# RMSNorm on one core: the second tile loaded in halves, the third stored whole, seven rows a group on GpSimd, one ScalarE table

## The chip, the cores and the metric

One Trainium2 chip, one of its cores. The metric is device time in microseconds (us).

## The reference

```python
batch, seq, dim = 16, 1024, 512
x = randn(batch, seq, dim) float32;  gamma = ones(dim) float32
rms = sqrt(mean(x ** 2, axis=-1, keepdims=True) + 1e-5)
out = x / rms * gamma
```

The input is 33.55 MB and so is the output: 67.1 MB in all, with very little arithmetic per byte.

## The kernel before

The 16384 rows are four tiles of 128 partitions x 32 rows x 512 elements (8.4 MB each) in three slots on the chip; tile 3 goes into the slot of tile 0. Work is cut into groups of up to 16 rows. ScalarE squares a piece of a group, VectorE sums it, ScalarE takes the square root, VectorE the reciprocal. Then the rows are shared: GpSimd multiplies the last `share` rows by their factors and by gamma; ScalarE scales the others and VectorE multiplies these by gamma. SyncE issues all transfers, in program order, on one queue.

```python
    load(0, 0, 0, 8)
    # (gamma in five small pieces)
    load(0, 0, 8, 16)
    load(0, 0, 16, 32)
    load(1, 1, 0, 32)
    # ...
    groups = [                         # tile, first row, rows, pieces, share of GpSimd
        (0, 0, 7, (7,), 2),
        (0, 7, 9, (4, 5), 4),
        (0, 16, 16, (7, 5, 4), 7),
        (1, 0, 16, (7, 5, 4), 8),
        (1, 16, 16, (7, 5, 4), 8),
        (2, 0, 16, (7, 5, 4), 8),
        (2, 16, 16, (7, 5, 4), 7),
        (3, 0, 16, (7, 5, 4), 7),
        (3, 16, 16, (7, 5, 4), 3),
    ]
    # ...
    def transfers(t, g):               # issued when a group's code is through
        if (t, g) == (0, 0):
            store(0, 0, 0, 1)
            load(2, 2, 0, 16)
            store(0, 0, 1, 2)
            load(2, 2, 16, 24)
            store(0, 0, 2, 3)
            load(2, 2, 24, 32)
        elif (t, g) == (0, 16):
            store(0, 0, 3, 16)
            store(0, 0, 16, 32)
            load(3, 0, 0, 16)
            load(3, 0, 16, 32)
        elif (t, g) == (1, 16):
            store(1, 1, 0, 32)
        elif (t, g) == (2, 0):
            store(2, 2, 0, 16)
        elif (t, g) == (2, 16):
            store(2, 2, 16, 32)
        elif (t, g) == (3, 0):
            store(3, 0, 0, 16)
        elif (t, g) == (3, 16):
            store(3, 0, 16, 32)
    # ...
    for k, group in enumerate(groups):
        # ... (mine = rows not given to GpSimd, half = half of them, ahead = the next group)
        scale_by_pool(rstd, t, g, n, share)
        for piece in todo[:2]:         # squares and sums of the next group
            square_sums(*piece)
        scale(rstd, t, g, 0, half)
        if not ahead:
            times_gamma(t, g, 0, half)
        for piece in todo[2:]:
            square_sums(*piece)
        scale(rstd, t, g, half, mine)
        times_gamma(t, g, 0 if ahead else half, mine)
        transfers(t, g)
        for nxt in ahead:
            rstd = inverse_rms(ss, nxt[2])
```

## Time and profile before

| | before |
|---|---|
| time, median of the first 3 runs | 161.52 us |
| span of the profiled run | 159.6 us |
| traffic | 67.1 MB, 421 GB/s over the span |
| busiest compute engine | VectorE, 70% |
| transfer engines | 98.2% |

The prediction below shows the busy shares, the stretches, the issues and the chain of waits. Three further readings: The first is SyncE's own waits before it issues (who waited for whom: us in total, times, longest):

```profile
SPq L49 <- DVE slot L115: 52.2, 7, 20.5
SPq L49 <- POOL slot L103: 36.0, 5, 9.2
SPq L45 <- DMA out_dram<-slot: 20.8, 2, 11.1
```

SyncE waits most of the time, for VectorE and GpSimd before stores and for landed stores before loads.

The second is the timeline of SyncE, the stores that matter (start us, duration, line and operation): the first small store, tile 1's, both halves of tile 2's, both of tile 3's.

```profile
27.13 0.35 SPq L49 DMA_DIRECT2D out_dram<-slot  x1
...
92.12 0.34 SPq L49 DMA_DIRECT2D out_dram<-slot  x1
...
108.02 0.34 SPq L49 DMA_DIRECT2D out_dram<-slot  x1
...
121.99 0.33 SPq L49 DMA_DIRECT2D out_dram<-slot  x1
...
135.98 0.33 SPq L49 DMA_DIRECT2D out_dram<-slot  x1
...
142.18 0.33 SPq L49 DMA_DIRECT2D out_dram<-slot  x1
```

The third is the longest wait of a compute engine:

```profile
POOL slot L102 <- DVE ss L96: 32.7, 4, 16.0
```

GpSimd stands 32.7 us, four times, until VectorE has its factors: 16.0 us at the start, and 6.9 us before tile 1, because ScalarE cannot square tile 1 until all 8.4 MB of it have landed.

### The profile page before, as it was taken

To read this page: it belongs to the slowest core of one execution; us is meant where nothing else is said; L and a number is where in the kernel's file an instruction comes from. 1 tells how busy PE (TensorE), PEld (TensorE's weight loads), DVE (VectorE), ACT (ScalarE), POOL (GpSimd) and SP (SyncE) were. 2 spreads that over 40 slices of the span, in tenths; PEclk is the share of its full clock that TensorE was granted. 3 is DMA by queue.
4 is the path that set the end of the run, shared out by engine and by line. 5 is a ranking of instruction groups with operands and counts; after the bars stand their busy time and mean duration, and the time that the engine had idled before them with its cause. 6 is when DMAs were issued, how large, how long until landed. Compare 5 with 4: busy or idle time off the path is not lost.

```text
span 159.6 us, 280 instructions
## 1 busy us (share of the span) xinstructions
PE 2.0 (1%) x2; PEld 0.5 (0%) x2; DVE 111.8 (70%) x43; ACT 108.5 (68%) x110; POOL 108.2 (68%) x24
## 2 busy tenths in 40 slices
PE   0050000000000000000000000000000000000000
PEld 0010000000000000000000000000000000000000
DVE  0027298998069899999999999999999809700000
ACT  3072999960499997989989989999995198000000
POOL 1000731981999309999999999999999999960000
DMA  5999999969799999999999999996999999999995
GB/s 199 419 435 485 435 394 526 526 263 526 329 394 396 454 415 419 427 452 444 476 394 402 509 402 394 526 526 263 526 394 394 394 501 419 394 452 468 394 419 238
DMA packets 2747, 67.12 MB, mean 421 GB/s; under 512 B 313, under 2 KB 314, under 8 KB 698
## 3 DMA queue, kind: packets, MB, share of 16 engines
q1 hardware_dynamic: 2746, 67.11, 98.2%
q14 instruction: 1, 0.01, 0.0%
HBM read 33.56 MB, written 33.55 MB: 421 GB/s over the span
## 4 chain that ended last, share of the span: by engine, by line
POOL 49%; DMA 26%; ACT 8%; DVE 3%; POOLq 2%; issue 0%
POOL slot L103 26%; DMA slot<-in_x_dram 26%; POOL slot L102 23%; ACT slot L111 3%; DVE slot L115 3%; ACT sq_psum L89 3%; POOLq L205 2%; ACT sq_sbuf L89 1%; DVE ss L96 0%; POOLq L102 0%
## 5 line engine op out<-in xcount | busy, mean ns | idle before, releaser
L102 POOL TENSOR_TENSOR slot<-slot,ss 128x3584 f32<-128x3584 f32 (+4 forms) x9 | 47.8, 5310 | 32.7 <-DVE ss L96 32.7
L90 DVE TENSOR_REDUCE ss<-sq_psum 128x7 f32<-128x3584 f32 (+1 forms) x16 | 49.1, 3066 | 20.1 <-ACT sq_psum L89 20.1
L103 POOL TENSOR_TENSOR slot<-slot,gamma_b 128x3584 f32<-128x3584 f32 (+4 forms) x9 | 60.2, 6692 | 0.7
L111 ACT ACTIVATE slot<-slot,ss 128x512 f32<-128x512 f32 x74 | 46.8, 707 | 4.7 <-DVE ss L96 4.7
L89 ACT ACTIVATE sq_psum<-slot 128x3584 f32<-128x3584 f32 (+1 forms) x16 | 40.2, 2510 | 12.4 <-DMA slot<-in_x_dram 11.0
L115 DVE TENSOR_TENSOR slot<-slot,gamma_psum 128x4608 f32<-128x4608 f32 (+4 forms) x10 | 40.8, 4093 | 4.9 <-ACT slot L111 4.9
L90 DVE TENSOR_REDUCE ss<-sq_sbuf 128x5 f32<-128x2560 f32 x8 | 22.4, 2805 | 0.0
L89 ACT ACTIVATE sq_sbuf<-slot 128x2560 f32<-128x2560 f32 x8 | 18.6, 2323 | 0.0
L95 ACT ACTIVATE ss<-ss,eps_t 128x16 f32<-128x16 f32 (+2 forms) x9 | 2.7, 303 | 4.2 <-DVE ss L90 4.2
L95 ACT ACT_TABLE_LOAD x1 | 1.3, 1283 | 4.0 <-DVE ss L90 4.0
L96 DVE RECIPROCAL ss<-ss 128x16 f32<-128x16 f32 (+2 forms) x9 | 2.1, 235 | 1.7 <-ACT ss L95 1.7
L65 PE MATMUL gamma_psum<-gamma_row,ones_col 1*128 1x512 f32 x2 | 2.0, 1118 | 8.7 <-DMA gamma_row<-in_gamma_dram 8.7
L89 ACT ACT_TABLE_LOAD x1 | 1.3, 1283 | 1.1 <-PEq L194 1.1
L160 ACT COPY gamma_b<-gamma_psum 128x512 f32<-128x512 f32 x1 | 0.6, 566 | 0.0
L65 PEld LDWEIGHTS gamma_psum<-gamma_row,ones_col 1*128 1x128 f32 x2 | 0.5, 308 | 8.7 <-issue 8.7
L63 POOL MEMSET ones_col<- 1x128 f32 x1 | 0.2, 194 | 0.3 <-POOLq L194 0.3
L194 POOL MEMSET const-float32-0.0<- 128x1 f32 x1 | 0.1, 98 | 0.2 <-issue 0.2
L194 POOL MEMSET const-bfloat16-1.0<- 128x1 bf16 x1 | 0.1, 101 | 0.0
L194 POOL MEMSET const-uint8-127<- 128x1 uint8 x1 | 0.1, 101 | 0.0
L194 POOL MEMSET const-float32-1.0<- 128x1 f32 x1 | 0.1, 98 | 0.0
L69 POOL MEMSET eps_t<- 128x1 f32 x1 | 0.1, 88 | 0.0
## 6 DMA issues: line engine op xcount, KB each, us to landing
out_dram<-slot SPq DMA_DIRECT2D x5, 4096.0 KB, 16.6
slot<-in_x_dram SPq DMA_DIRECT2D x4, 4096.0 KB, 19.3
slot<-in_x_dram SPq DMA_DIRECT2D x4, 2048.0 KB, 9.9
out_dram<-slot SPq DMA_DIRECT2D x1, 3328.0 KB, 32.4
out_dram<-slot SPq DMA_DIRECT2D x3, 256.0 KB
gamma_row<-in_gamma_dram SPq DMA_DIRECT2D x4, 0.4 KB
gamma_row<-in_gamma_dram SPq DMA_DIRECT2D x1, 0.5 KB
slot<-in_x_dram SPq DMA_DIRECT2D x1, 34.3
```

The source lines that it names most:

```text
L65: nc.tensor.matmul(gamma_psum[:, 0], ones_col, gamma_row, start=True, stop=True)
L89: nc.scalar.activation(out=sq[:, :m], in_=rows, func=AF.Square)
L90: nc.vector.tensor_reduce(out=ss[:, r : r + m, 0], in_=sq[:, :m], axis=mybir.AxisListType.X, op=OP.add)
L95: nc.scalar.activation(out=ss[:, :n, 0], in_=ss[:, :n, 0], func=AF.Sqrt, bias=eps_t, scale=1.0 / D)
L96: nc.vector.reciprocal(out=ss[:, :n, 0], in_=ss[:, :n, 0])
L102: nc.gpsimd.tensor_tensor(out=part, in0=part, in1=by_row, op=OP.mult)
L103: last = nc.gpsimd.tensor_tensor(out=part, in0=part, in1=gamma_b.to_broadcast([P, share, D]), op=OP.mult)
L111: nc.scalar.activation(out=x[:, g + r, :], in_=x[:, g + r, :], func=AF.Copy, scale=rstd[:, r])
L115: scaled = nc.vector.tensor_tensor(out=part, in0=part, in1=gamma_psum.to_broadcast([P, r1 - r0, D]), op=OP.mult)
L160: nc.scalar.copy(out=gamma_b[:, 0], in_=gamma_psum[:, 0])
L194: nc = _bacc.Bacc("TRN2", target_bir_lowering=False, num_devices=1)
L205: with _tile.TileContext(nc) as tc:
```

## The change

The intent, read from the diff: let compute start on tile 1 when half of it is there; balance GpSimd (15.9 us for a group with eight rows) with VectorE; load ScalarE's table once, in idle time; and with that room spend fewer, larger transfers and instructions (tile 2 stored whole, the last group's multiply in one piece).

```diff
--- before.py
+++ after.py
@@ -57,7 +57,8 @@
         nc.sync.dma_start(out=gamma_row[:, c0:c1], in_=gamma.unsqueeze(0)[:, c0:c1])
     load(0, 0, 8, 16)
     load(0, 0, 16, 32)
-    load(1, 1, 0, 32)
+    load(1, 1, 0, 16)
+    load(1, 1, 16, 32)
 
     ones_col = const.tile([1, P], fp32)
     nc.gpsimd.memset(ones_col, 1.0)
@@ -67,15 +68,17 @@
 
     eps_t = const.tile([P, 1], fp32)
     nc.gpsimd.memset(eps_t, eps)
+    table = const.tile([P, 1], fp32)
+    nc.scalar.activation(out=table, in_=eps_t, func=AF.Sqrt)
 
 
     groups = [
-        (0, 0, 7, (7,), 2),
-        (0, 7, 9, (4, 5), 4),
+        (0, 0, 7, (7,), 3),
+        (0, 7, 9, (4, 5), 5),
         (0, 16, 16, (7, 5, 4), 7),
-        (1, 0, 16, (7, 5, 4), 8),
-        (1, 16, 16, (7, 5, 4), 8),
-        (2, 0, 16, (7, 5, 4), 8),
+        (1, 0, 16, (7, 5, 4), 7),
+        (1, 16, 16, (7, 5, 4), 7),
+        (2, 0, 16, (7, 5, 4), 7),
         (2, 16, 16, (7, 5, 4), 7),
         (3, 0, 16, (7, 5, 4), 7),
         (3, 16, 16, (7, 5, 4), 3),
@@ -134,10 +137,8 @@
             load(3, 0, 16, 32)
         elif (t, g) == (1, 16):
             store(1, 1, 0, 32)
-        elif (t, g) == (2, 0):
-            store(2, 2, 0, 16)
         elif (t, g) == (2, 16):
-            store(2, 2, 16, 32)
+            store(2, 2, 0, 32)
         elif (t, g) == (3, 0):
             store(3, 0, 0, 16)
         elif (t, g) == (3, 16):
@@ -168,12 +169,10 @@
         for piece in todo[:2]:
             square_sums(*piece)
         scale(rstd, t, g, 0, half)
-        if not ahead:
-            times_gamma(t, g, 0, half)
         for piece in todo[2:]:
             square_sums(*piece)
         scale(rstd, t, g, half, mine)
-        times_gamma(t, g, 0 if ahead else half, mine)
+        times_gamma(t, g, 0, mine)
         transfers(t, g)
         for nxt in ahead:
             rstd = inverse_rms(ss, nxt[2])
```

## The prediction

> **What bounds the kernel now.** I read the page's head first, then the stretches, then the DMA queue's own issues and waits, and only last the chain of waits, which here points at the wrong thing.
>
> The page's busy shares, its slices and the DMA totals:
>
> ```profile
> PE 2.0 (1%) x2; PEld 0.5 (0%) x2; DVE 111.8 (70%) x43; ACT 108.5 (68%) x110; POOL 108.2 (68%) x24
> DMA  5999999969799999999999999996999999999995
> q1 hardware_dynamic: 2746, 67.11, 98.2%
> HBM read 33.56 MB, written 33.55 MB: 421 GB/s over the span
> ```
>
> No compute engine passes 70%; the transfer engines are at 98.2%. The two 5s are the first and last slice. The 6s and 7s need a second look, because this row books a packet in the slice where it starts, and a 64 KB packet takes 2.4 us of a 4 us slice. So I asked for busy time by stretch (columns: stretch in us and its length, then each engine's busy time, the clock, the DMA share, GB/s):
>
> ```profile
> 0.00:1.70 1.70, 0.00 (x0) 0.00 (x0) 0.00 (x0) 0.55 (x1) 0.43 (x6) 1.00 0.00 0
> 1.70:158.40 156.70, 2.04 (x2) 0.50 (x2) 111.83 (x43) 107.94 (x110) 107.79 (x18) 1.00 1.00 428
> 158.40:159.60 1.20, 0.00 (x0) 0.00 (x0) 0.00 (x0) 0.00 (x0) 0.00 (x0) 1.00 0.00 0
> ```
>
> From 1.7 us to 158.4 us the share is 1.00: the queue is never dry. The span is 1.7 us until the first packet, 156.7 us of moving 67.11 MB at 428 GB/s, and 1.2 us until the last landing is seen. The profiled run took 161.61 us, 2.0 us more than its 159.6 us span. That is the whole time; no engine is in it.
>
> How far ahead is the queue filled? The issues, with the median time from issue to landing at the right:
>
> ```profile
> out_dram<-slot SPq DMA_DIRECT2D x5, 4096.0 KB, 16.6
> slot<-in_x_dram SPq DMA_DIRECT2D x4, 4096.0 KB, 19.3
> out_dram<-slot SPq DMA_DIRECT2D x1, 3328.0 KB, 32.4
> ```
>
> 4 MiB (4.19 MB) at 428 GB/s is 9.8 us. A store that lands 16.6 us after its issue has stood some 7 us behind others, so issuing it some us later costs nothing.
>
> The chain of waits says something else:
>
> ```profile
> by line: POOL slot L103 26.4%; DMA slot<-in_x_dram 26.0%; POOL slot L102 22.5%; ACT slot L111 3.5%; DVE slot L115 3.1%; ACT sq_psum L89 3.1%; POOLq L205 2.2%; ACT sq_sbuf L89 1.4%; issue 0.3%; DVE ss L96 0.1%; POOLq L102 0.1%
> ```
>
> It follows the last *engine* instruction, a GpSimd multiply that ends at 142.2 us, while the program ends at 159.6 us. Its 49% of GpSimd describes a chain whose output then waits in the queue.
>
> **What the Trainium skill says.** "DMA: Bandwidth & Descriptors", Specifications, gives a fabric ceiling of 435 GB/s for a core's 16 engines. The trace agrees: 428 GB/s over 156.7 us. The same page, Queues, rings and completion order, says that each engine consumes descriptors in ring order; I use this as first-in first-out. "ScalarE: Activation LUTs", What ACT_TABLE_LOAD costs, gives about 1283 ns a load plus a drain; the trace shows two loads of exactly 1283 ns. "GPSIMD Engine Reference", section 3.1, gives 4497 ns for a two-input [...]operation of 2048 fp32 a partition against 2293 ns on VectorE; here the multiply by gamma of that size takes 4513 ns, but the one with the row factor broadcast only 3601 ns, so I use the trace's rows.
>
> **The change part by part.** The rows used (engine operation, form, count, busy, mean ns):
>
> ```profile
> L103 POOL TENSOR_TENSOR slot<-slot,gamma_b 128x4096 f32<-128x4096 f32 x3 | 26.6, 8870 | 0.2
> L103 POOL TENSOR_TENSOR slot<-slot,gamma_b 128x3584 f32<-128x3584 f32 x3 | 23.3, 7776 | 0.2
> L102 POOL TENSOR_TENSOR slot<-slot,ss 128x4096 f32<-128x4096 f32 x3 | 21.0, 7015 | 6.9 <-DVE ss L96 6.9
> L102 POOL TENSOR_TENSOR slot<-slot,ss 128x3584 f32<-128x3584 f32 x3 | 18.5, 6166 | 3.8 <-DVE ss L96 3.8
> L95 ACT ACT_TABLE_LOAD x1 | 1.3, 1283 | 4.0 <-DVE ss L90 4.0
> ```
>
> To see what is on the path I need deadlines: when the queue reaches each transfer. With all bytes ahead of it at 2.335 us per MB (156.7/67.11) from 1.7 us on: the first small store at 41 us (16.8 MB of loads ahead); tile 1's store at 99.6 (41.9 MB); tile 2's at 119.2 (50.3 MB); its second half at 129.0; tile 3's two stores at 138.8 and 148.6. Before, their issues stand in the SyncE timeline at 27.1, 92.1, 108.0, 122.0, 136.0 and 142.2 us: margins of 14, 7.5, 11, 7, 2.8 and 6.4 us, all positive, which is why nothing is dry.
>
> 1. Table. One of two loads goes from the path of the first group (1.28 us) to the idle time before the first data (7.9 us). With three instead of two rows given to GpSimd the first VectorE multiply has four rows instead of five (0.54 us a row). First store issued at about 25 instead of 27.1; deadline 41. Worth 0.
> 2. Tile 1 in halves. ScalarE's square of tile 1 waited until the whole 8 MB landed at 42.2 us. The first half, 12.6 MB in, lands at about 32. ScalarE finishes the preceding work at 36.7, so it saves 5.5 us there, and the reciprocal for tile 1 comes at about 54 instead of 59.9. In bytes nothing changes. The trace's packet records give 2418 ns for 64 KB and 1213 ns for 32 KB: a transfer engine needs 16 x 1213 instead of 8 x 2418 ns, +0.06 us. All transfers are numbered one higher; SyncE issued the ninth only when the first had landed (at 7.9 us), so I read eight semaphores used in turn. The transfers now sharing one lie eight apart and have landed long before. Worth +0.06.
> 3. Seven rows on GpSimd. A group of eight costs 7.02 + 8.87 = 15.9 us, of seven 6.17 + 7.78 = 13.9 us, 2.0 less in each of three groups. VectorE's multiply gains a row, 4.95 instead of 4.41 us; its start-to-start period goes from 13.15 to 13.69 us (the seven-row stretch 99.5 to 113.2 shows it), still below GpSimd. So with tile 1's first reciprocal at 54, GpSimd ends groups at about 68, 82, 96, 110 and 124 us. Tile 1's store is issued at 82 instead of 92.1: it only stands longer. Worth 0.
> 4. Tile 2 stored whole. It must wait for the second half: issued at about 110, against 108.0 for the first half before. Deadline 119.2, margin 9. Packets of 64 KB instead of 32: -0.06 us.
> 5. The last group unsplit. ScalarE's 13 rows take 8.07 us, then VectorE's multiply 7.1 in one, no longer overlapped: issue at about 139 if the group starts at 124; deadline 148.6. Worth 0.
>
> Sum on the path: +0.06 - 0.06 = 0.00. One small chance remains: the last 64 KB packets of tile 1's load took 2785 instead of 2418 ns in the packet records (at 38.7 to 41.6 us, 0.37 us lost on every engine). I don't know the cause; with 32 KB packets it may halve. I allow -0.1: 161.5 - 0.1 = 161.4 us.
>
> **The rivals.** *Compute sets the end.* The chain's reading would give 5.9 (first half) + 3 x 2.0 (seven rows) + about 1.3 (table) = 13 us saved, 148 us. Against it: 67.11 MB at even the page's 435.2 GB/s is 154.2 us, and with the 1.7, 1.2 and 2.0 us outside 159.1 us (an estimate from that page and the trace). No schedule of this traffic is over 1.5% faster.
>
> *The whole store starves the queue.* Had compute kept its pace, the store of tile 2 would be issued at 122.0, 2.8 us after its deadline, plus some 1 us until the first packet (0.74 to 1.75 us at the start): 165.3 us, 2.4% slower. The parts 2 and 3 are there to prevent it. Even if the early half brought nothing, 60.2 + 4 x 14.0 = 116 us still meets 119.2. So both would have to fail.
>
> *The last group becomes the bound.* If it started as before (reciprocal at 126.9), the unsplit end comes at 126.9 + 8.1 + 7.2 = 142.2 us, as before. It would have to slip by 6.4 us to cost anything.
>
> **Range and chances.** Three runs before lie within 0.13 us. The transfers' slow packets and another chip may move it some tenths. 161.4 us, eight times in ten 160.9 to 161.9. Over 2% faster needs 158.3 us or less, below the 159.1 us floor: 0.01. Over 2% slower needs 164.8, about 3.3 us of dry queue, which only the second rival makes, with 9 us of margin against it: 0.01. Within 2%: 0.98.
>
> **What would show it.** Right: the DMA share is again 1.00 from about 1.7 us to the last packet at about 158.3; the gap of 6.9 us before GpSimd's multiply in tile 1 shrinks or goes; one table load, early; tile 1's store issued near 82, landing some 38 us later; tile 2's near 110, landing near 139; the last near 139. Wrong: a stretch of low DMA share near 119 us with SyncE waiting for GpSimd or VectorE there, a second table load between first squares and square root that reaches the first store, or a DMA rate other than 428 GB/s. A time under 159 us would mean that the traffic has another ceiling than I read.

## The result, and the profile after

| | before | after |
|---|---|---|
| time, median of 4 runs each | 161.54 us (161.43 to 161.66) | 161.56 us (161.45 to 161.56) |
| span of the profiled run | 159.6 us | 159.5 us |

The ratio is 0.9999, 95% interval 0.9982 to 1.0017. A ratio is the mean time of one kernel's runs over that of the other's of the same rounds, so not quite the ratio of the medians quoted. The time is the same.

The stretches of the changed kernel, same columns as in the prediction:

```profile
0.00:1.70 1.70, 0.00 (x0) 0.00 (x0) 0.00 (x0) 0.55 (x1) 0.44 (x6) 1.00 0.00 0
1.70:158.40 156.70, 2.04 (x2) 0.49 (x2) 112.55 (x42) 107.60 (x111) 105.96 (x18) 1.00 1.00 428
158.40:159.60 1.20, 0.00 (x0) 0.00 (x0) 0.00 (x0) 0.00 (x0) 0.00 (x0) 1.00 0.00 0
```

The middle stretch is the same 156.7 us at share 1.00 and 428 GB/s. What did change is all in front of the queue. SyncE's timeline, the same stores (tile 2's is one now):

```profile
24.91 0.35 SPq L49 DMA_DIRECT2D out_dram<-slot  x1
...
82.15 0.39 SPq L49 DMA_DIRECT2D out_dram<-slot  x1
...
109.18 0.34 SPq L49 DMA_DIRECT2D out_dram<-slot  x1
...
123.16 0.33 SPq L49 DMA_DIRECT2D out_dram<-slot  x1
...
138.00 0.33 SPq L49 DMA_DIRECT2D out_dram<-slot  x1
```

Tile 1's store is issued 10.0 us sooner, tile 3's first 12.8 us, the last 4.2 us. None of it reaches the end. The last store shows where it goes, issue to landing in us at the right, after:

```profile
out_dram<-slot SPq DMA_DIRECT2D x1, 4096.0 KB, 20.7
```

Before, the last store was issued at 142.18 us and took 16.6 us; 142.18 + 16.6 = 158.8. Now 138.00 + 20.7 = 158.7. The 4.2 us won are spent standing in the queue. The waits of the engines, after:

```profile
POOL slot L105 <- DVE ss L99: 21.7, 4, 14.7
...
ACT sq_psum L92 <- DMA slot<-in_x_dram: 7.0, 2, 5.3
```

GpSimd's wait fell by 11.0 us. ScalarE's table load, two before, is one, in idle time (from the costliest groups):

```profile
L72 ACT ACT_TABLE_LOAD x1 | 1.3, 1283 | 1.1 <-PEq L193 1.1
```

ScalarE waits for data 7.0 us instead of 11.0, and one of its two waits is new: 1.73 us at 91.1 us, for the load of tile 3. Compute has run so far ahead that it now catches up with the loads. The chain of waits has changed entirely: it gave GpSimd 49% before, and none of its 44 pieces is GpSimd's now, while the time is the same.

### The profile page after: what moved, and what is told of

The parts are those of the page before. It is cut to its first block, busy times and chain, and to the rows that moved or that the text cites. A ratio compares the mean times of both kernels' runs of the same rounds, so it can differ in the third digit from the quotient of the medians.

```text
span 159.5 us, 280 instructions
## 1 busy us (share of the span) xinstructions
PE 2.0 (1%) x2; PEld 0.5 (0%) x2; DVE 112.5 (71%) x42; ACT 108.2 (68%) x111; POOL 106.4 (67%) x24
## 4 chain that ended last, share of the span: by engine, by line
DMA 38%; DVE 29%; ACT 16%; issue 2%; ACTq 0%; SPq 0%
DMA out_dram<-slot 22%; DMA slot<-in_x_dram 17%; DVE ss L93 17%; DVE slot L118 12%; ACT slot L114 8%; ACT sq_psum L92 6%; ACT sq_sbuf L92 1%; ACTq L204 0%; ACT ss L98 0%; ACT gamma_b L161 0%; DVE ss L99 0%; SPq L49 0%; ACTq L92 0%
## 5 line engine op out<-in xcount | busy, mean ns | idle before, releaser
L105 POOL TENSOR_TENSOR slot<-slot,ss 128x3584 f32<-128x3584 f32 (+2 forms) x9 | 46.9, 5216 | 21.7 <-DVE ss L99 21.7
L106 POOL TENSOR_TENSOR slot<-slot,gamma_b 128x3584 f32<-128x3584 f32 (+2 forms) x9 | 59.2, 6582 | 0.7
L114 ACT ACTIVATE slot<-slot,ss 128x512 f32<-128x512 f32 x75 | 47.5, 709 | 4.7 <-DVE ss L99 4.7
L118 DVE TENSOR_TENSOR slot<-slot,gamma_psum 128x4608 f32<-128x4608 f32 (+2 forms) x9 | 41.3, 4592 | 8.5 <-ACT slot L114 8.5
```

What stands on the lines that cost most here:

```text
L105: nc.gpsimd.tensor_tensor(out=part, in0=part, in1=by_row, op=OP.mult)
L106: last = nc.gpsimd.tensor_tensor(out=part, in0=part, in1=gamma_b.to_broadcast([P, share, D]), op=OP.mult)
L114: nc.scalar.activation(out=x[:, g + r, :], in_=x[:, g + r, :], func=AF.Copy, scale=rstd[:, r])
L118: scaled = nc.vector.tensor_tensor(out=part, in0=part, in1=gamma_psum.to_broadcast([P, r1 - r0, D]), op=OP.mult)
```

## The experiments

The theory: the transfer queue sets the end. Each transfer has a deadline, the moment at which the queue has finished all before it; an issue well before its deadline costs nothing, one after it costs the lateness plus the time from issue to first packet. Rival 1: the chain of engine work (mostly GpSimd) sets the end. Rival 2: the whole store is harmless in any case, and the other parts have no purpose. Twelve kernels were run: four that do parts of the change alone (a1, a2, a3, d1), three that change GpSimd's work (a4, b4, b3), four with less traffic (b1, b2, c1, c2), and one that changes the order of transfers (c3). The ratio given is to the kernel before in the same rounds.

### a1: tile 2 stored whole, alone

```diff
 # the kernel before
-        elif (t, g) == (2, 0):
-            store(2, 2, 0, 16)
         elif (t, g) == (2, 16):
-            store(2, 2, 16, 32)
+            store(2, 2, 0, 32)
```

> The kernel before with one part of the change alone: tile 2 stored whole after its second half. Theory (the transfer queue sets the end, every transfer has a deadline): compute is as slow as before, so the store is issued at about 122.0 us, while the queue finishes tile 1's store at about 119.4 us; with some 1 us from issue to first packet the queue is dry for about 3.6 us and the time is about 165.1 us (2.2% slower), with a dip in the DMA row near 119 us. Rival 1 (the chain of GpSimd work sets the end): GpSimd does what it did, so 161.5 us. Rival 2 (a whole store is hidden anyway): 161.5 us.

Measured: 165.27 us, ratio 1.0221 (1.0205 to 1.0236), slower. The stretches, and the issue of tile 2's store in SyncE's timeline:

```profile
1.70:119.20 117.50, 2.04 (x2) 0.49 (x2) 96.65 (x38) 97.10 (x93) 84.72 (x14) 1.00 1.00 428
119.40:122.50 3.10, 0.00 (x0) 0.00 (x0) 3.10 (x3) 2.54 (x5) 3.10 (x2) 1.00 0.00 0
122.60:162.20 39.60, 0.00 (x0) 0.00 (x0) 11.78 (x4) 8.07 (x13) 19.68 (x4) 1.00 0.98 424
```

```profile
122.28 0.34 SPq L49 DMA_DIRECT2D out_dram<-slot  x1
```

The packet records (start and length of every packet in the trace) show no transfer from 119.97 to 123.13 us: 0.84 us pass from the issue to the first packet. A dry stretch of 3.2 us in the queue goes with a time 3.6 us longer (165.27 - 161.69). Most of the last 0.4 us is in the packet records too: after the dry stretch the remaining 16.8 MB took 39.0 us, here and in a4 below, and 38.7 us in the kernel before, where the queue did not have to start again. Both rivals said 161.5 us and fall. GpSimd did what it did before, and the kernel is slower.

### a2: whole store and seven rows

```diff
 # a1, and
-        (1, 0, 16, (7, 5, 4), 8),
-        (1, 16, 16, (7, 5, 4), 8),
-        (2, 0, 16, (7, 5, 4), 8),
+        (1, 0, 16, (7, 5, 4), 7),
+        (1, 16, 16, (7, 5, 4), 7),
+        (2, 0, 16, (7, 5, 4), 7),
```

> The kernel before with tile 2 stored whole and seven instead of eight rows on GpSimd in the three groups that had eight; no early half of tile 1, no table part. Theory (queue and deadlines): GpSimd starts tile 1 at about 60.2 us and takes 14.0 us a group, so the store is issued at about 116.2 us, 3 us before the queue is through with tile 1's store: 161.5 us. Rival 1 (GpSimd chain sets the end): about 155.5 us, 2 us less for each of three groups.

Measured: 161.60 us, ratio 1.0014 (0.9972 to 1.0056), the same (one of its four runs took 162.99 us). The store of tile 2 was issued at 116.72 us, 5.6 us sooner than in a1.

### a3: whole store and tile 1 in halves

```diff
 # a1, and
-    load(1, 1, 0, 32)
+    load(1, 1, 0, 16)
+    load(1, 1, 16, 32)
```

> The kernel before with tile 2 stored whole and tile 1 loaded in two halves; GpSimd keeps eight rows. Theory (queue and deadlines): GpSimd starts tile 1 at about 54.5 us and takes three groups of 15.9 us and one of 14.0 us, so the store is issued at about 116.3 us, 3 us before it is needed: 161.5 us. Rival 1 (GpSimd chain sets the end): about 156 us, as the chain starts 5.9 us sooner.

Measured: 161.63 us, ratio 0.9994 (0.9977 to 1.0011), the same. Issue at 116.67 us, again 5.6 us sooner than a1. Either of the two parts is enough to pay for the whole store; together they leave room. (Neither part was run without the whole store; that it is then worth nothing follows from the theory and was not measured.)

### d1: the remaining parts alone

```diff
 # the kernel before
+    table = const.tile([P, 1], fp32)
+    nc.scalar.activation(out=table, in_=eps_t, func=AF.Sqrt)
-        (0, 0, 7, (7,), 2),
-        (0, 7, 9, (4, 5), 4),
+        (0, 0, 7, (7,), 3),
+        (0, 7, 9, (4, 5), 5),
-        if not ahead:
-            times_gamma(t, g, 0, half)
-        times_gamma(t, g, 0 if ahead else half, mine)
+        times_gamma(t, g, 0, mine)
```

> The kernel before with the remaining parts of the change alone: the early table load, three and five rows on GpSimd in the first two groups, and the last group's multiply in one piece; tile 1 is loaded whole, tile 2 stored in two halves, eight rows stay on GpSimd elsewhere. Theory (queue and deadlines): one table load instead of two, the first small store issued at about 24.9 instead of 27.1 us, where it isn't needed until 41 us; the last store is issued at about 142.2 us, as before, 6 us before it is needed: 161.5 us. Rival 1 (the chain of engine work sets the end): the 2 us gained at the start come out, 159.5 us, or the unsplit multiply costs its 3 us, 164.5 us.

Measured: 161.55 us, ratio 0.9999 (0.9982 to 1.0015), the same. The first small store is issued at 25.13 us, 2.0 us sooner than before; the last store at 142.14 us, as before.

### a4 and b4: spending the margin on purpose

```diff
 # the changed kernel; groups (1, 0), (1, 16), (2, 0), (2, 16)
-        (1, 0, 16, (7, 5, 4), 7),
+        (1, 0, 16, (7, 5, 4), 9),    # a4; 8 in b4; likewise in the other three
```

> The changed kernel with nine instead of seven rows on GpSimd in tile 1's and tile 2's groups: the margin of tile 2's store is used up on purpose. Theory (queue and deadlines): a group costs GpSimd about 17.9 us, from 53.1 us on four of them end at about 124.7 us, 5.3 us after the queue is through with tile 1's store; with 1 us to the first packet the time is about 167.8 us (3.9% slower), not the 15.6 us that the four groups become longer. Rival 1 (GpSimd chain sets the end): about 177 us.

> The changed kernel with eight instead of seven rows on GpSimd in tile 1's and tile 2's groups. Theory (queue and deadlines): four groups of 15.9 us from 53.1 us end at about 116.8 us, 2.6 us before the queue needs the store: 161.5 us, although GpSimd's groups are 7.8 us longer in sum. Rival 1 (GpSimd chain sets the end): about 169 us.

Measured: nine rows 167.59 us, ratio 1.0368 (1.0352 to 1.0383), slower; eight rows 161.43 us, ratio 0.9974 (0.9946 to 1.0002), the same. SyncE's issue of tile 2's store, in the timeline of b4 and then of a4, and the dry stretch of a4:

```profile
116.97 0.34 SPq L49 DMA_DIRECT2D out_dram<-slot  x1
```

```profile
124.60 0.34 SPq L49 DMA_DIRECT2D out_dram<-slot  x1
```

```profile
119.40:124.90 5.50, 0.00 (x0) 0.00 (x0) 1.83 (x2) 3.63 (x6) 5.50 (x2) 1.00 0.00 0
```

Against the changed kernel's 109.18 us, eight rows cost 7.8 us of GpSimd time and nothing of the end; nine rows cost 15.4 us and 5.9 us of the end (167.59 - 161.69, the kernel before in the same rounds). The packet records of a4 show the queue empty from 119.78 to 125.44 us, 5.7 us. So the curve is flat up to an issue at 116.97 us. Between a1 and a4, run in the same rounds, the issue comes 2.32 us later and the time is 2.32 us longer: slope one. No run has an issue between 117.0 and 122.3 us, so the corner itself was not measured; as 0.84 us pass before the first packet, it must lie that much before the deadline, at about 119 us (an estimate). The deadline itself, 119.8 to 120.0 us, is nearly the same in a1 and a4; the prediction had worked out 119.2.

### b3: GpSimd's multiply by gamma left out

```diff
 # the changed kernel (gamma is one here, so the output stays right; not a valid kernel)
-        nc.gpsimd.tensor_tensor(out=part, in0=part, in1=by_row, op=OP.mult)
-        last = nc.gpsimd.tensor_tensor(
-            out=part, in0=part, in1=gamma_b.to_broadcast([P, share, D]), op=OP.mult
-        )
+        last = nc.gpsimd.tensor_tensor(out=part, in0=part, in1=by_row, op=OP.mult)
```

> The changed kernel without GpSimd's multiply by gamma (59 us of GpSimd work less; gamma is one in these inputs, so that the output stays right here, but it is no valid kernel). Theory (queue sets the end): 161.5 us, the DMA share stays 1.00 from 1.7 to 158.4 us. Rival 1 (the chain of engine work sets the end): over 5 us less.

Measured: 161.62 us, ratio 0.9986 (0.9958 to 1.0014), the same. Its middle stretch (GpSimd's busy time, 46.92 us, stands just before the clock), and GpSimd's longest wait:

```profile
1.70:158.40 156.70, 2.04 (x2) 0.49 (x2) 112.53 (x42) 107.54 (x111) 46.92 (x9) 1.00 1.00 428
```

```profile
POOL slot L105 <- DVE ss L99: 70.1, 8, 14.9
```

59 us of GpSimd work are gone, and the queue's share and rate are the same (1.00 and 428 GB/s): here GpSimd's work did not slow the transfers. But b3 is a weak test of rival 1. GpSimd now waits 70.1 us for VectorE's factors (21.7 in the changed kernel), and tile 2's store is issued at 108.84 us, only 0.3 us sooner, the last one at 137.90, 0.1 us sooner: VectorE, with 13.7 us a group against GpSimd's 14.0, held the pace, so compute hardly ended sooner. What rules out a chain of compute as the end is the changed kernel itself (last store 4.2 us sooner, nothing gained), a2 and a3 (5.6 us sooner than in a1, and only a1's 3.6 us came back) and b4 (7.8 us later, nothing lost).

### b1 and b2: less traffic

If the queue hides the gain, a lighter queue must show it. Both kernels without one store:

```diff
         elif (t, g) == (0, 16):
             store(0, 0, 3, 16)
-            store(0, 0, 16, 32)      # wrong output on purpose: these rows are never written
             load(3, 0, 0, 16)
```

> The kernel before without the store of tile 0's second half (4.19 MB less traffic; part of the output is wrong on purpose). Theory (queue and deadlines): every later transfer could move up by 9.8 us, but the issues for tile 1, the halves of tile 2 and tile 3 come at 92.1, 108.0, 122.0, 136.0 and 142.2 us; the store of tile 3's first half at 136.0 us finds the queue dry, so the end is 136.0 + 1.0 + 2 x 9.8 + 1.2 = 157.8 us of span and about 159.8 us of time: only 1.8 of the 9.8 us come out. A kernel bound by its queue alone would take 151.7 us; a kernel bound by compute alone 161.5 us.

> The changed kernel with the same cut (tile 0's second half is not stored, wrong on purpose). Theory (queue and deadlines): its issues at 82.2, 109.2, 122.5 and 138.0 us all meet the earlier deadlines but for a dry stretch of some 1.6 us before tile 3's load, so the time is about 154.3 us, 3.5% below the kernel before with the same cut: the gain in compute that the full traffic hides. Rival (the change gains nothing in compute worth having): as the kernel before with the cut, about 159.8 us.

Measured: the kernel before with the cut 159.73 us, the changed one with the cut 155.66 us. Their outputs are wrong, as meant. The change is now worth 4.1 us (155.75/159.73 by the means: 2.5%). Stretches of the kernel before with the cut:

```profile
71.30:72.50 1.20, 0.00 (x0) 0.00 (x0) 1.20 (x1) 1.20 (x2) 1.20 (x1) 1.00 0.00 0
122.40:122.90 0.50, 0.00 (x0) 0.00 (x0) 0.50 (x1) 0.00 (x0) 0.50 (x1) 1.00 0.00 0
132.90:136.90 4.00, 0.00 (x0) 0.00 (x0) 4.00 (x2) 2.28 (x4) 4.00 (x2) 1.00 0.00 0
```

Three dry stretches, the longest right before tile 3's first store, issued at 136.13 us. With the change only the first is left (tile 3's load must wait until tile 0's rows have landed outside); behind it the queue of b2 runs to its end:

```profile
72.70:152.30 79.60, 0.00 (x0) 0.00 (x0) 55.91 (x20) 49.69 (x57) 56.31 (x10) 1.00 0.99 419
```

b2's rival (no gain in compute worth having) falls. But I had expected 154.3 us for b2, 1.4 us less. In its packet records the last packets of tile 3's load, at 90 to 92.4 us, took longer, 1.27 us on the mean transfer engine; this accounts for the size of the miss, and its cause is open. With full traffic the same place loses 0.2 us or less.

### c1 and c2: what two parts are worth where compute matters

```diff
 # b2 (the changed kernel, lighter traffic), and
 # c1:
-    load(1, 1, 0, 16)
-    load(1, 1, 16, 32)
+    load(1, 1, 0, 32)
 # c2, in groups (1, 0), (1, 16), (2, 0):
-        (1, 0, 16, (7, 5, 4), 7),
+        (1, 0, 16, (7, 5, 4), 8),
```

> The changed kernel with the lighter traffic (tile 0's second half not stored, wrong on purpose), and tile 1 loaded whole again: what the early half is worth where compute matters. With the lighter traffic the changed kernel took 155.7 us, and its queue was through with tile 1's store at about 112.5 to 113.5 us. Theory (queue and deadlines): without the early half tile 2's store is issued 5.9 us later, at about 115.1 us instead of 109.2, so the queue is dry until about 116.0 us and the time is 116.0 + 38.9 (16.8 MB) + 1.2 + 2.0 = about 158.1 us. Rival (the early half never matters): 155.7 us.

> The changed kernel with the lighter traffic (wrong on purpose), and eight instead of seven rows on GpSimd in the three groups that had eight before. Theory (queue and deadlines): the groups end at 53.1 + 3 x 15.9 + 14.0 = 114.9 us, so tile 2's store is 5.7 us later and the time about 157.9 us, where with the full traffic eight rows cost nothing. Rival (seven rows never matter): 155.7 us.

Measured: c1 159.41 us, c2 157.93 us, against 155.66 us for b2 (another chip; the kernel before took 161.60 and 161.65 us beside them). Tile 2's store was issued at 116.21 us in c1 and 115.10 us in c2, against 109.24 us in b2. Both parts matter where the traffic is lighter. c2 is as expected. c1 is 1.3 us over, and 1.1 of it is the early half: it moves tile 2's store by 7.0 us, not 5.9. The traces show why. With the table load gone and more rows on GpSimd in the first groups, ScalarE was ready for tile 1 at 35.2 us in the changed kernel, not at 36.7 us as before, so a whole load holds it longer: in c1 it stood 6.65 us (until 42.16), where it had stood 5.56 us in the kernel before.

### c3: all loads first

The changed kernel's queue still loses some tenths at about 38 us, when tile 1's load ends and the first small store begins. I tried to take that switch away:

```diff
 # the changed kernel
     load(1, 1, 16, 32)
+    load(2, 2, 0, 32)
 # (the three small stores and tile 2's three loads at (0, 0) are gone)
-            store(0, 0, 3, 16)
+            store(0, 0, 0, 16)
```

> The changed kernel with full traffic, tile 2's load as one transfer right behind tile 1's, and the first sixteen rows of tile 0 stored as one transfer after it (three small stores of 256 KB gone, so one switch of the queue from loads to stores less). Theory (the queue sets the end, and its only losses are packets that take longer at such switches, 0.3 us near 38 us, and the short packets of the small stores, some 0.15 us): about 161.1 us, 0.3% less, not over 0.6%. Rival (those losses do not come from the switch or are taken again elsewhere): 161.5 us.

Measured: 162.56 us, ratio 1.0066 (1.0050 to 1.0083): 0.7% slower where I had expected 0.3% less, clear of noise. Stretches:

```profile
1.70:58.00 56.30, 2.04 (x2) 0.49 (x2) 41.17 (x18) 43.53 (x41) 34.60 (x7) 1.00 1.00 429
58.00:62.00 4.00, 0.00 (x0) 0.00 (x0) 4.00 (x2) 3.65 (x5) 3.92 (x2) 1.00 1.12 352
62.00:158.00 96.00, 0.00 (x0) 0.00 (x0) 67.46 (x24) 60.30 (x66) 67.45 (x11) 1.00 1.00 433
158.20:160.30 2.10, 0.00 (x0) 0.00 (x0) 0.00 (x0) 0.00 (x0) 0.00 (x0) 1.00 0.04 16
```

(A share above 1 only means that packets are booked where they start.) The loss has moved and grown: at the first of the two switches left, from tile 2's load to tile 0's store, the last sixteen 64 KB packets took 1.22 us longer on the mean, and at the end the last two packets ended 1.2 us after the others. (The profiled run, 163.42 us, is the slowest of its six, so the second part need not be in all of them.) My reading of those tenths as a loss to be saved is wrong. Why a switch costs 0.3 us in one place and 1.2 in another stays open. No version with the whole output beats the two kernels beyond the noise.

## Why the prediction was right

It said 161.4 us, 160.9 to 161.9; measured 161.56 us.

- **The bound.** A queue with share 1.00 from 1.7 to 158.4 us: the line is the same after, with a last store issued 4.2 us sooner, and in b4, with tile 2's store 7.8 us later. The chain of waits, which gave GpSimd 49%, was rightly set aside.
- **Deadlines and margins.** Tile 2's whole store: issue predicted near 110 us, measured 109.18; deadline 119.2, measured 119.8 to 120.0. Tile 1's store: 82, measured 82.15. This agreement is partly luck: GpSimd was through at 81.2 us, but SyncE issues in program order and stood until 81.72 us at tile 3's second load, which waited for a store to land; in b2, without that wait, the issue came at 81.24 us. The last store: 139, measured 138.00. The second rival named what would break it; a1 made it happen, 165.27 us where the prediction had 165.3. The size is partly luck: the dry stretch was 3.2 us where the prediction had 2.8 + 1 = 3.8, and two things that it did not have made up for it: the 0.3 us of starting again, and 161.69 instead of 161.5 us for the kernel before in those rounds.
- **Parts 2 and 3 together keep the whole store in time.** a2 and a3 show that one would do, as the prediction said of part 3. The issue moved from 122.28 us (a1) by 5.6 with seven rows and by 5.6 with the halves; 122.28 - 5.6 - 5.6 = 111.1, and the remaining 1.9 us to 109.18 agree with d1's first store, 2.0 us sooner.
- **Mis-sized: tile 1's reciprocal "at about 54 instead of 59.9".** It came at 52.8 us. Parts 1 and 2 were sized apart, and the earlier start of part 1 makes part 2 worth more: 7.0 us in c1, where the prediction had 5.5 to 5.9.
- **Not foreseen: ScalarE's wait for tile 3's load,** 1.73 us at 91.1 us. It is off the path.
- **The allowance of 0.1 us** for slower packets at the end of tile 1's load: their loss was 0.37 us before and 0.31 us after, in one trace each; the time did not show it. c3 makes me doubt that such a loss can be read as something to save.

## What to carry to other kernels

Where the transfer queue is busy from its first packet to its last, work out for each transfer when the queue will reach it, and compare this with its issue: only an issue that comes too late for that moment moves the end, and then by its lateness plus the time to the first packet (0.84 us here). A chain of waits that follows the last compute instruction says nothing of the end if the program ends with queued transfers, and a long wait at an issue is not yet a gap. Work that readies a store sooner, as the early half and the seven rows each do by 5.6 us, may show nothing in the time and still be what makes another part (here the whole store) free; to see what it is worth, lighten the traffic.

## What the Trainium skill lacked or had wrong

- "DMA: Bandwidth & Descriptors", Latency and other measured facts, gives some 600 ns to the first byte for transfers issued by SyncE. Here 0.84 us passed from the start of the issue to the first packet when the queue was dry (122.28 to 123.13 and 124.60 to 125.44 us), and 0.50 us from the end of the 0.34 us that SyncE's issue took. The page does not say from where it counts, so these runs don't show it wrong.
- The same page, as far as I read it, has nothing on the switch from loads to stores in one full queue: the last packets of the load took longer, by 0 to 0.6 us in most places and by 1.2 to 1.3 us on the mean transfer engine in b2, c1, c2 and c3. The cause is open.
- "GPSIMD Engine Reference", section 3.1, has one duration for a two-input operation, an add: 4497 ns at 2048 fp32 a partition. The multiply by gamma took nearly the same (4513 ns), but the one whose second input is one factor a row, broadcast, took 3601 ns.
- No page that I read warns of a view that ends with the last compute instruction while transfers go on for 17 us; here it named GpSimd for 49% of the span before the change and not at all after it, at the same time.
